# Rotary embedding on one core: first store of 4 and 12 rows, and a load that waits for a multiplication

## The chip, the core and the metric

The kernel runs on one core of a Trainium2 chip. The metric is the device time of one execution in microseconds (us). Three runs of the kernel before gave 161.43, 161.47 and 161.59 us; their median is 161.47.

## What is computed

`x` has shape (16, 512, 16, 64) in float32: batch, sequence, heads, dim. `cos` and `sin` have shape (512, 32), one row for each place in the sequence. Only the first 32 of the 64 numbers are turned, with the first 16 columns of `cos` and `sin`; the other 32 pass through.

```
x1, x2 = x[..., :32], x[..., 32:]
first  = x1[..., :16] * cos[..., :16] - x1[..., 16:] * sin[..., :16]
second = x1[..., :16] * sin[..., :16] + x1[..., 16:] * cos[..., :16]
out    = concatenate([first, second, x2])
```

All of `x` is read once and all of `out` is written once, 33.55 MB each.

## The kernel before

The 8192 positions (batch times sequence) are cut into T = 4 tiles. Each tile gives every one of the 128 partitions K = 16 consecutive rows (positions) of 16 heads by 64 numbers, so that one partition of a tile is 64 KB of contiguous memory and a tile is 8 MB. A ring of NS = 3 tiles (L46) lies in on-chip memory; tile t uses place t % 3, and a tile is worked where it lies and stored from there. Tile 3 therefore takes the place of tile 0, and its load waits until the stores of tile 0 have landed.

`load` (L55) and `store` (L58) each issue one DMA for rows `lo` to `hi` of a tile. All go through SP's queue (`nc.sync`), in the order of the program, but for the tables (L64, L65) and the store of tile 2 (L136), which POOL issues. A DMA issue that must wait stops what stands behind it on the same queue.

At the start the tables go out, then the loads of tile 0, tile 1 and rows 8 to 15 of tile 2 (L66 to L68). VectorE (DVE in the profile) spreads the tables over the partitions (L74 to L86). Then `rotate` (L91) works pieces of tiles, all on VectorE. For rows `lo` to `hi` it issues four instructions: the product with sin into `b_t` (L97), the product with cos in place (L98), the subtraction for the first quarter (L99) and the addition for the second (L106). With `cut`, the addition is issued in two pieces, so that something can wait for the first of them. It returns the subtraction and the list of additions.

`hold` (L114) makes a transfer wait for one VectorE instruction, beyond what its data need.

The order of the work (L124 to L141): tile 0 in two halves of 8 rows (KC = 8), the second with the addition cut after row 11 (KP = 12). The store of tile 0's first half waits for that first piece of the addition; the store of its second half follows, then the load of tile 2's rows 0 to 7, and the load of tile 3. Tile 1 is worked in two halves and stored; that store waits for the subtraction `near` of tile 2's rows 0 to 4 (KM = 5). Tile 2 is worked rows 8 to 15 first, then rows 0 to 4, then rows 5 to 7, and stored by POOL. Tile 3 is worked in two halves and stored.

Of the kernel before, what the change touches and what calls it, by code (L numbers as in the profile page):

```python
# [1 line left out]

# [4 lines left out]


@with_exitstack
def kernel(  # L10
    ctx: ExitStack,
    tc: tile.TileContext,
    x: bass.AP,
    cos: bass.AP,
    sin: bass.AP,
    out: bass.AP,
):
    nc = tc.nc
    fp32 = mybir.dt.float32
    P = 128  # L20
    B, S, H, D = x.shape
    Q = D // 4
    HF = D // 2

    K = 16
    T = B * S // (P * K)
    PB = S // K
    REP = P // PB  # L30
    R = H * D
    NS = 3
    KC = K // 2
    KM = 5
    KP = K - 4

    xf = x.rearrange("b s h d -> (b s h d)").rearrange("(t p f) -> t p f", t=T, p=P)
    of = out.rearrange("b s h d -> (b s h d)").rearrange("(t p f) -> t p f", t=T, p=P)
    cosf = cos.rearrange("(p k) j -> p (k j)", k=K)
    sinf = sin.rearrange("(p k) j -> p (k j)", k=K)  # L40

    const_pool = ctx.enter_context(tc.tile_pool(name="const", bufs=1))
    b_pool = ctx.enter_context(tc.tile_pool(name="bp", bufs=1, space=bass.MemoryType.PSUM))


    ring = const_pool.tile([P, NS, K, H, D], fp32)  # L46
    stage = const_pool.tile([P, 2, K, HF], fp32)
    spun = const_pool.tile([P, 2 * K, Q], fp32)
    packed = const_pool.tile([PB, 2 * K, Q], fp32)
    table = const_pool.tile([P, 2, K, 2, Q], fp32)  # L50

    def rows(t, lo, hi):
        return ring[:, t % NS, lo:hi].rearrange("p k h d -> p (k h d)")

    def load(t, lo=0, hi=K):  # L55
        return nc.sync.dma_start(out=rows(t, lo, hi), in_=xf[t, :, lo * R : hi * R])

    def store(t, lo=0, hi=K, queue=nc.sync):  # L58
        return queue.dma_start(out=of[t, :, lo * R : hi * R], in_=rows(t, lo, hi))  # L59


    nc.vector.memset(stage[:, :, :, 0:Q], 0.0)  # L62
    spread = stage.rearrange("(j b) t k i -> j b t (k i)", b=REP)
    nc.gpsimd.dma_start(out=spread[:, 0, 0], in_=cosf)  # L64
    nc.gpsimd.dma_start(out=spread[:, 0, 1], in_=sinf)  # L65
    load(0)  # L66
    load(1)
    load(2, KC, K)  # L68

    PQ = PB // REP
    nc.vector.stream_shuffle(  # L74
        out=spun[:],
        in_=stage.rearrange("p t k j -> p (t k) j")[:, :, 0:Q],
        mask=[j % PQ * REP for j in range(PB)],
    )
    for q in reversed(range(REP)):
        n = PQ * (q + 1)  # L80
        nc.vector.tensor_copy(out=packed[0:n], in_=spun[q * PB : q * PB + n])  # L81

    for r in range(REP):
        nc.vector.tensor_copy(  # L84
            out=table[r * PB : (r + 1) * PB].rearrange("p t k c j -> p (t k) c j"),
            in_=packed.unsqueeze(2).to_broadcast((PB, 2 * K, 2, Q)),  # L86
        )
    C = table[:, 0].rearrange("p k c j -> p k (c j)")
    Sn = table[:, 1].rearrange("p k c j -> p k (c j)")

    def rotate(t, lo, hi, cut=None):  # L91
        x1 = ring[:, t % NS, lo:hi, :, 0:HF]
        c = C[:, lo:hi].unsqueeze(2).to_broadcast((P, hi - lo, H, HF))
        s = Sn[:, lo:hi].unsqueeze(2).to_broadcast((P, hi - lo, H, HF))
        b_full = b_pool.tile([P, KC, H, HF], fp32, name="b_t")
        b_t = b_full[:, 0 : hi - lo]
        nc.vector.tensor_mul(out=b_t, in0=x1, in1=s)  # L97
        nc.vector.tensor_mul(out=x1, in0=x1, in1=c)  # L98
        first = nc.vector.tensor_sub(  # L99
            out=x1[:, :, :, 0:Q], in0=x1[:, :, :, 0:Q], in1=b_t[:, :, :, Q:HF]  # L100
        )
        ends = [hi - lo] if cut is None else [cut - lo, hi - lo]
        done = []
        for a, b in zip([0] + ends, ends):
            done.append(
                nc.vector.tensor_add(  # L106
                    out=x1[:, a:b, :, Q:HF],
                    in0=x1[:, a:b, :, Q:HF],
                    in1=b_t[:, a:b, :, 0:Q],
                )  # L110
            )
        return first, done

    def hold(transfer, point):  # L114
        tc.add_manual_dep(
            transfer.ins,
            point.ins.name,
            mybir.DependencyInfo(
                mybir.DependencyClass.Sync, mybir.DependencyReason.DATA
            ),  # L120
            reason="the store follows the loads at the DMA engines",
        )

    rotate(0, 0, KC)  # L124
    _, close = rotate(0, KC, K, cut=KP)
    hold(store(0, 0, KC), close[0])
    store(0, KC, K)
    load(2, 0, KC)
    load(3)
    rotate(1, 0, KC)  # L130
    rotate(1, KC, K)
    behind_loads = store(1)
    rotate(2, KC, K)
    near, _ = rotate(2, 0, KM)
    rotate(2, KM, KC)
    store(2, queue=nc.gpsimd)  # L136

    hold(behind_loads, near)
    rotate(3, 0, KC)
    rotate(3, KC, K)  # L140
    store(3)  # L141


# [1 line left out]
_INS = ['x', 'cos', 'sin']  # L145
_OUTS = [((16, 512, 16, 64), 'float32')]


# [23 lines left out]
```

## Time and profile before

| what | us |
|---|---|
| median of three runs | 161.47 |
| the profiled execution | 161.67 |
| its span, first to last instruction | 159.8 |
| VectorE busy | 113.0 |
| end of VectorE's last addition | 131.3 |
| last store, issue to landing | 27.5 |

The profiled execution's time is 1.87 us longer than its span; the difference is what lies around the first and the last instruction. HBM is read for 33.69 MB and written for 33.55 MB, a mean of 421 GB/s over the span.

How to read the profile: in the timeline a line has the start, the duration, the engine (SPq is SP's queue of DMA issues), the line of the kernel, the operation, the tile written and the tile read with their shapes, and how many instructions were merged. A DMA issue's line is the issuing alone; the transfer goes on after it, and its landing is told separately. In the queue table a line has the number of packets, the MB and the share of 16 engines' span that the packets took.

### The profile page before, as it was taken

How to read it: one execution, taken by the hardware profiler on the slowest of the kernel's cores; microseconds unless marked ns; L12 is line 12 of the kernel's file. 1: busy time of each engine (PE TensorE's matmuls, PEld its weight loads, DVE VectorE, ACT ScalarE, POOL GpSimd, SP SyncE). 2: the span in 40 equal slices, each digit the busy share in tenths (PEclk: the TensorE clock that was granted, in tenths of full speed). 3: DMA queues.
4: the chain of work that ended last, by engine and by line, in shares of the span. 5: the costliest groups of instructions: out<-in, count | busy, mean ns of one | idle time of the engine just before them, and what ended most of it. 6: DMA issues, size and time to landing. Idle time of an engine off the chain costs nothing.

```text
span 159.8 us, 120 instructions
## 1 busy us (share of the span) xinstructions
DVE 113.0 (71%) x48; POOL 1.9 (1%) x7
## 2 busy tenths in 40 slices
DVE  1000959999999999999999999999999980000000
POOL 3000000000000000000000000010000000000000
DMA  7969989899799999999999799996996996996990
GB/s 262 541 262 541 410 377 525 377 410 525 303 467 410 394 484 426 402 402 508 402 525 476 312 525 394 394 525 295 492 525 262 525 508 279 525 508 279 525 508 16
DMA packets 1504, 67.24 MB, mean 421 GB/s; under 512 B 192, under 2 KB 192, under 8 KB 224
## 3 DMA queue, kind: packets, MB, share of 16 engines
q1 hardware_dynamic: 1296, 58.72, 85.4%
q0 software_dynamic: 208, 8.52, 12.3%
HBM read 33.69 MB, written 33.55 MB: 421 GB/s over the span
## 4 chain that ended last, share of the span: by engine, by line
DVE 61%; DMA 14%; issue 5%; DVEq 1%
DVE b_t L97 22%; DVE ring L98 22%; DMA ring<-in_x_dram 14%; DVE ring L106 10%; DVE ring L99 7%; DVEq L167 1%; DVEq L97 0%
## 5 line engine op out<-in xcount | busy, mean ns | idle before, releaser
L97 DVE TENSOR_TENSOR b_t<-ring,table 128x4096 f32<-128x4096 f32 (+2 forms) x9 | 35.6, 3958 | 2.1 <-DMA ring<-in_x_dram 1.9
L98 DVE TENSOR_TENSOR ring<-ring,table 128x4096 f32<-128x4096 f32 (+2 forms) x9 | 35.6, 3950 | 0.3
L99 DVE TENSOR_TENSOR ring<-ring,b_t 128x2048 f32<-128x2048 f32 (+2 forms) x9 | 18.4, 2050 | 0.3
L106 DVE TENSOR_TENSOR ring<-ring,b_t 128x2048 f32<-128x2048 f32 (+3 forms) x10 | 18.4, 1853 | 0.0
L74 DVE LOAD_MASK_SELECT spun<-stage x1 | 0.0, 14 | 14.4 <-DMA stage<-in_sin_dram 14.4
L84 DVE COPY table<-packed 32x1024 f32<-32x1024 f32 x4 | 2.7, 684 | 0.1
L59 POOL DMA_DIRECT2D out_dram<-ring x1 | 0.6, 562 | 101.8 <-DVE ring L106 101.8
L81 DVE COPY packed<-spun 32x512 f32<-32x512 f32 (+3 forms) x4 | 1.7, 416 | 0.1
L62 DVE MEMSET stage<- 128x512 f32 x1 | 0.5, 485 | 0.9 <-PEq L156 0.9
L74 DVE STREAM_SHUFFLE spun<-stage 128x512 f32<-128x512 f32 x1 | 0.7, 721 | 0.0
L64 POOL DMA_DIRECT2D stage<-in_cos_dram x1 | 0.6, 644 | 1.3 <-DVE stage L62 1.3
L65 POOL DMA_DIRECT2D stage<-in_sin_dram x1 | 0.5, 535 | 0.0
L156 POOL MEMSET const-bfloat16-1.0<- 128x1 bf16 x1 | 0.1, 102 | 0.0
L156 POOL MEMSET const-float32-0.0<- 128x1 f32 x1 | 0.1, 99 | 0.2 <-issue 0.2
L156 POOL MEMSET const-float32-1.0<- 128x1 f32 x1 | 0.1, 99 | 0.0
L156 POOL MEMSET const-uint8-127<- 128x1 uint8 x1 | 0.1, 99 | 0.0
## 6 DMA issues: line engine op xcount, KB each, us to landing
ring<-in_x_dram SPq DMA_DIRECT2D x2, 4096.0 KB, 40.8
out_dram<-ring SPq DMA_DIRECT2D x2, 4096.0 KB, 17.4
stage<-in_cos_dram POOLq DMA_DIRECT2D x1, 64.0 KB, 9.0
stage<-in_sin_dram POOLq DMA_DIRECT2D x1, 64.0 KB, 13.4
ring<-in_x_dram SPq DMA_DIRECT2D x3, 28.9
out_dram<-ring SPq DMA_DIRECT2D x2, 31.1
out_dram<-ring POOLq DMA_DIRECT2D x1, 39.6
```

The lines of the kernel that those rows point to most:

```text
L59: return queue.dma_start(out=of[t, :, lo * R : hi * R], in_=rows(t, lo, hi))
L62: nc.vector.memset(stage[:, :, :, 0:Q], 0.0)
L64: nc.gpsimd.dma_start(out=spread[:, 0, 0], in_=cosf)
L65: nc.gpsimd.dma_start(out=spread[:, 0, 1], in_=sinf)
L74: nc.vector.stream_shuffle(out=spun[:], in_=stage.rearrange("p t k j -> p (t k) j")[:, :, 0:Q], mask=[j % PQ * REP for j in range(PB)],)
L81: nc.vector.tensor_copy(out=packed[0:n], in_=spun[q * PB : q * PB + n])
L84: nc.vector.tensor_copy(out=table[r * PB : (r + 1) * PB].rearrange("p t k c j -> p (t k) c j"), in_=packed.unsqueeze(2).to_broadcast((PB, ...
L97: nc.vector.tensor_mul(out=b_t, in0=x1, in1=s)
L98: nc.vector.tensor_mul(out=x1, in0=x1, in1=c)
L99: first = nc.vector.tensor_sub(out=x1[:, :, :, 0:Q], in0=x1[:, :, :, 0:Q], in1=b_t[:, :, :, Q:HF])
L106: nc.vector.tensor_add(out=x1[:, a:b, :, Q:HF], in0=x1[:, a:b, :, Q:HF], in1=b_t[:, a:b, :, 0:Q],)
L167: with _tile.TileContext(nc) as tc:
```

## The change

The first store of tile 0 carries 4 rows (KS = 4) and the second 12, instead of 8 and 8; what the first one waits for stays as it is. The load of tile 2's rows 0 to 7, which is next in SP's queue, is made to wait for the product with cos (the line that is L98 before) of tile 1's rows 8 to 12. For that, tile 1's second half is worked as 5 and 3 rows, and `rotate` returns this product too. Tile 2's rows 0 to 7 are worked as 4 and 4 rows instead of 5 and 3, and the store of tile 1 waits for the subtraction of the 4 rows.

```diff
+    KS = 4
...
-        nc.vector.tensor_mul(out=x1, in0=x1, in1=c)
+        scaled = nc.vector.tensor_mul(out=x1, in0=x1, in1=c)
...
-        return first, done
+        return scaled, first, done
...
     rotate(0, 0, KC)
-    _, close = rotate(0, KC, K, cut=KP)
-    hold(store(0, 0, KC), close[0])
-    store(0, KC, K)
-    load(2, 0, KC)
+    _, _, close = rotate(0, KC, K, cut=KP)
+    hold(store(0, 0, KS), close[0])
+    store(0, KS, K)
+    behind_store = load(2, 0, KC)
     load(3)
     rotate(1, 0, KC)
-    rotate(1, KC, K)
+    near, _, _ = rotate(1, KC, KC + KM)
+    hold(behind_store, near)
+    rotate(1, KC + KM, K)
     behind_loads = store(1)
     rotate(2, KC, K)
-    near, _ = rotate(2, 0, KM)
-    rotate(2, KM, KC)
+    _, near, _ = rotate(2, 0, KS)
+    rotate(2, KS, KC)
     store(2, queue=nc.gpsimd)

     hold(behind_loads, near)
```

## The prediction

> **What bounds the kernel now.** I read the page's busy table first, then its slices, its queue table, the chain, the timeline, SP's own waits, and last the trace's DMA packet records (start, duration and size of each packet).
>
> ```profile
> DVE 113.0 (71%) x48; POOL 1.9 (1%) x7
> ...
> DMA  7969989899799999999999799996996996996990
> ...
> q1 hardware_dynamic: 1296, 58.72, 85.4%
> q0 software_dynamic: 208, 8.52, 12.3%
> ```
>
> The reader is to see that VectorE (DVE) stops at about four fifths of the span, while the two DMA queues together hold 85.4 + 12.3 = 97.7% of 16 engines' time: 0.977 x 159.8 = 156.1 us. The dips in the slices are an artefact of counting a packet where it starts. In the packet records every engine runs packet on packet, the first beginning at 1.75 us and the last ending at 158.44; the last landing is at 158.80 and the span ends 1.0 later. A 64 KB packet takes 2.418 us and a 32 KB one 1.212, reading or writing. So the DMA engines set the end, and the chain on the page, which follows VectorE, misleads: VectorE is done at 131.3 and the last store still needs 27.5 us to land.
>
> ```profile
> 47.64 2.34 DVE L106 TENSOR_TENSOR ring<-ring,b_t 128x1024 f32<-128x1024 f32 x2
> 48.88 1.47 SPq L59 DMA_DIRECT2D out_dram<-ring  x2
> ...
> 50.40 21.85 SPq L56 DMA_DIRECT2D ring<-in_x_dram  x2
> ...
> 63.46 4.43 DVE L97 TENSOR_TENSOR b_t<-ring,table 128x4096 f32<-128x4096 f32 x1
> 67.93 4.42 DVE L98 TENSOR_TENSOR ring<-ring,table 128x4096 f32<-128x4096 f32 x1
> ...
> 76.91 4.43 DVE L97 TENSOR_TENSOR b_t<-ring,table 128x4096 f32<-128x4096 f32 x1
> ...
> 90.35 2.83 DVE L97 TENSOR_TENSOR b_t<-ring,table 128x2560 f32<-128x2560 f32 x1
> 93.22 2.83 DVE L98 TENSOR_TENSOR ring<-ring,table 128x2560 f32<-128x2560 f32 x1
> ...
> 104.44 4.43 DVE L97 TENSOR_TENSOR b_t<-ring,table 128x4096 f32<-128x4096 f32 x1
> ```
>
> This is the timeline around the change. SP sends the two halves of tile 0 from 48.88, the first half of tile 2's load at 50.40, and then stands until 71.9, where tile 3's load goes. The other answer to read is SP's waits:
>
> ```profile
> SPq L56 <- DMA out_dram<-ring: 20.1, 1, 20.1
> ```
>
> Tile 3's load waits 20.1 us for tile 0's stores to land, because it takes their place in the ring of tiles.
>
> Where each transfer ended at the DMA engines (its 4-byte completion packets), for a middle engine and for the last one:
>
> ```
>                       middle   last
> load 2, rows 8-15      51.41   51.86
> store 0, rows 0-7      61.11   61.54
> store 0, rows 8-15     70.88   71.23
> load 2, rows 0-7       80.56   80.96
> load 3                 99.88  100.48
> store 3               157.84  158.44
> ```
>
> By following packet ends into packet starts, the last one is the same engine from 51.86 on; it alone decides. It loses time against the plain packet sum twice: the last packet of load 2 takes 1.458 instead of 1.212 (+0.246, 50.40 to 51.86), the last of load 3 takes 2.596 instead of 2.418 (+0.178, 97.89 to 100.49). Both are changes from reading memory to writing it. At the one change from writing to reading (69.3 to 71.0) it loses nothing, but five leading engines take 1.48 to 1.62 for their last 32 KB written, +0.26 to +0.40, mean 0.33. Those still end ahead of it, so that costs nothing now.
>
> **The change part by part.**
>
> *4 and 12 rows.* Each engine still writes 16 packets: 8 of 16 KB and 8 of 48 KB for 16 of 32 KB. Two 32 KB packets take 2 x 1.212 = 2.424, one of 64 KB 2.418, so a packet costs some 0.006 of its own, and an equal count gives 0. Bounds: 0, and 8 x 0.006 = 0.05 if rows of 48 KB go as two packets. The issue times stay at 48.88 and 50.0, since both waits stay. The smaller first store lasts 8 x 0.61 = 4.9 us from 51.1, the second is issued 1.1 us before that begins; hidden with 6.0 us to spare (1.1 + 4.9), beyond which each us late would be a us of gap.
>
> *The held load.* It waits for the 5-row L98 of tile 1's second half. The first L97 there starts at 63.46; in the 5 and 3 row tile of before, L98 ends 93.22 + 2.83 - 90.35 = 5.70 after such a start. So 69.16, and SP sends 0.03 later, as at 48.85 to 48.88: **69.19 instead of 50.40**. Behind it on SP are load 3, store 1 and store 3. Load 3 can't go before tile 0's stores land at 71.85, so it keeps its time; the others go at 97 and 131. The 1.39 us that SP spent on issuing this load at 50.40 go too, and are worth nothing: it stood until 71.9 anyway.
>
> The queue that was never empty now runs out about then. Without the +0.33 the engines would end tile 0's stores 16 x 1.212 + 0.01 after load 2: 70.49 to 70.99, the last at 71.24. When the first data of a newly sent load flow is shown only at the start: load 0 is issued at 0.74, its first packets begin at 1.75 to 2.84, and end, less 2.418, at 2.45 to 2.98. So 1.71 to 2.24 us from issue to flow, and here 70.90 to 71.43. For the last engine: 0 to 0.19 late, and I take its own start of then, 2.84 - 0.74 = 2.10, so 71.29 and **+0.06**.
>
> To it comes what the turn itself costs. Before, the read was queued 18 us ahead and five engines still lost 0.33; the last engine, turning when the others were already reading, lost none. Now nobody can read ahead, and all 16 turn within half a microsecond, the last among them. Bounds: 0 (as it is now for the last engine) and 0.84, the latter if the first packet's excess at the start (0.53 to 1.08, mean of 14 engines 0.84) comes on top of its latest arrival. I take the nearest row, the five engines that turn without their read in flow: **+0.33**.
>
> The Trainium skill, "DMA: Bandwidth & Descriptors", section "Latency and other measured facts", gives about 600 ns to the first byte of a transfer sent by SP. By that estimate the load would be there at 69.8, ahead of every engine's last write, and the sum would be 0; the row shows 1.01 us to the very first packet of this program and over 2 to the latest. The same page's "Rules for kernel authors" says to issue a DMA early and wait on it late, which speaks against holding a load back; no run shows yet what that is worth here.
>
> *Tile 1's second half as 5 and 3 rows.* Four VectorE instructions more. From the timeline, 8 rows in one take 90.35 - 76.91 = 13.44, as 5 and 3 rows 104.44 - 90.35 = 14.09: **+0.65 on VectorE** from 76.9 on. Tile 2's 4 and 4 for 5 and 3 is again eight instructions: 0. POOL's store 2 goes at 105.4, store 3 at 131.96. Both are hidden: at 131.3 each engine still has two to three packets of store 2, some 7 us, and the first packet of store 3 began only at 136.0. If that cover were gone, 0.65 would stand at the end. Data are in time: load 2's first half lands at 81.4 and is used at 91.0 (9.6 us spare), load 3 at 100.8, used at 105.1 (4.3 spare).
>
> *Store 1's wait.* It follows the subtraction of 4 rows rather than 5. With the mean of the 5 and 3 row forms (2.83 and 1.77; 1.49 and 0.95): 91.00 + 2.34 + 2.34 + 1.22 = 96.90 against 97.59. It lies behind load 3 until 99.8 either way: 0. Bounds -0.18 to +0.18, as the last engine's stall beside it could go or double.
>
> **Sum.** 0 + 0.06 + 0.33 + 0 + 0 = +0.39. The profiled execution took 161.67 us (span 159.8 and 1.87 around it), 0.20 over the median of the runs; so 162.06 for such an execution, and 161.47 + 0.39 = 161.86 for the median.
>
> **The rivals.**
>
> *On time.* The load arrives before the last engine needs it, and the turn costs that engine nothing, as before. For it: 0.06 is all that the start's rows ask, and leaders may lose up to 0.4 free. Against it: those rows are of an idle memory. 161.5, within 0.3.
>
> *The stall goes (the other side).* The +0.246 of the last engine lies from 50.40 to 51.86, exactly while SP pushes the load into a queue that takes it slowly (1.39 us rather than 0.34 to 0.42). If that push delays the engine, it is gone, and with it perhaps the 0.178 at 97.89, where store 1's issue falls. Price: -0.42, so 161.05; the next engines end 0.4 to 0.7 earlier than the last, so there is no more to get. It decides if the held load costs under 0.1. Against it: at 71.9 load 3's issue delays no engine by over 0.13, and the 0.178 needs a change 0.7 us early to matter.
>
> *A longer gap.* A load sent into full write traffic takes longer than in an idle memory. From 71.29 and 0.84 more: +0.06 + 0.84 = +0.90, 162.4. Store 1, issued at 97.59 and flowing at 99.8 without a gap, says that a store's part needs under 2.2; no row has a load so.
>
> *The wait holds nothing.* Not possible: SP stands at that load from 50.4, and the multiplication ends at 69.16.
>
> **How the numbers follow.** Forecast (a gap and turn of 0.33 to 0.6) 0.38; longer gap 0.08; on time 0.35; stall gone 0.19. A measurement of this kernel can tell about 0.2%, 0.32 us, from no change. Slower 0.38 + 0.08 = 0.46, same 0.35, faster 0.19. The range goes from the stall gone, 161.05, to the longer gap, 162.4; the forecast's own is 161.8 to 162.1.
>
> **What would show it.** In the packet records: the first packet of load 2's rows 0-7 lasting 1.5 us and more, and the last engine's end of that load at 81.3 instead of 80.96. In the timeline: SP's load at 69.2, VectorE's end at 131.9. I am wrong if the last engine passes 71.2 without a gap (on time), if its packet at 50.40 falls to 1.21 (stall gone), or if another engine comes last.

## The result and the profile after

The changed kernel takes 163.51 us in the median of six runs (162.97 to 165.29), beside 161.47 before: a ratio of 1.014, with a 95% interval of 1.011 to 1.017. It is slower, as forecast, but by 2.04 us in the medians and not by 0.39, and outside the range. Its times also spread over 2.3 us, where those before spread over 0.2.

The page of the changed kernel, the lines that answer to those shown of before:

```profile
DVE 113.5 (70%) x52; POOL 1.9 (1%) x7
...
DMA  7969969959999998899999699899899898899890
...
q1 hardware_dynamic: 1296, 58.72, 85.2%
q0 software_dynamic: 208, 8.52, 12.2%
```

The bound is the same: 85.2 + 12.2 = 97.4% of 161.4 us are 157.2 us of packets on each engine, 1.1 more than before (156.1) for the same bytes and the same number of packets. So the engines hardly stood empty more than before; some packets took longer.

SP's issues in the timeline (start, duration; two merged DMAs each), and what SP waited for:

```profile
48.83 1.48 SPq L60 DMA_DIRECT2D out_dram<-ring  x2
69.12 2.87 SPq L57 DMA_DIRECT2D ring<-in_x_dram  x2
96.85 35.41 SPq L60 DMA_DIRECT2D out_dram<-ring  x2
```

```profile
SPq L57 <- DVE ring L99: 18.8, 1, 18.8
SPq L57 <- DMA out_dram<-ring: 2.1, 1, 2.1
```

The load went at 69.12 (forecast 69.19) and store 1 at 96.85 (forecast 96.92): the order of events came as worked out. Tile 3's load waits 2.1 us instead of 20.1 and goes at 71.7 (71.9 before); the wait only changed its name.

Where the time is lost is seen by stretches. The columns are the stretch, its length, busy time of VectorE and POOL, the clock, the DMA share and GB/s; a packet counts whole where it starts. Before, then after:

```profile
70.50:75.00 4.50, 4.47 (x3) 0.00 (x0) 1.00 1.08 466
75.00:97.00 22.00, 21.79 (x8) 0.00 (x0) 1.00 0.99 429
97.00:101.50 4.50, 4.43 (x4) 0.00 (x0) 1.00 1.08 466
```

```profile
70.50:75.00 4.50, 4.43 (x4) 0.00 (x0) 1.00 1.03 386
75.00:97.00 22.00, 21.76 (x11) 0.00 (x0) 1.00 1.03 445
97.00:101.50 4.50, 4.43 (x3) 0.00 (x0) 1.00 1.16 451
```

The share tells how long the packets took, the GB/s how much they carried. Where the queue turns from tile 0's stores to the load (70.5 to 75), 466 GB/s fell to 386 at nearly the same share. Where it turns from load 3 to store 1 (97 to 101.5), the share rose from 1.08 to 1.16 while less was carried. Between the two (75 to 97) no packets were slow. In the packet records, with the ends told as in the prediction's table, the changed kernel has:

```
                      middle   last    against before
load 2, rows 0-7       81.12   81.69   +0.56  +0.73
load 3                100.92  101.78   +1.04  +1.30
store 3               158.88  159.74   +1.04  +1.30
```

The last engine lost 0.73 at the first turn, 0.57 more at the second and nothing afterwards. Of the profiled execution's own 163.22 - 161.67 = 1.55 us, 1.30 are thus placed; the other 0.25 lie behind the last completion. The first turn slowed not only the load's first packets but also its second ones (32 KB, 1.212 us elsewhere). Of the 16 first packets, which started at 70.6 to 71.1, 12 were slow by over 0.1 us, up to 0.97; of the 16 second ones 11 were, from 71.9 to 72.6, by up to 0.84. At the second, 15 of 16 last packets of load 3 were slow: 2.96 us in the mean, not 2.418.

### The profile page after: what moved, and what is told of

The parts are those of the page before. It is cut to its first block, busy times and chain, and to the rows that moved or that the text cites. A ratio compares the mean times of both kernels' runs of the same rounds, so it can differ in the third digit from the quotient of the medians.

```text
span 161.4 us, 123 instructions
## 1 busy us (share of the span) xinstructions
DVE 113.5 (70%) x52; POOL 1.9 (1%) x7
## 3 DMA queue, kind: packets, MB, share of 16 engines
q1 hardware_dynamic: 1296, 58.72, 85.2%
q0 software_dynamic: 208, 8.52, 12.2%
## 4 chain that ended last, share of the span: by engine, by line
DVE 62%; DMA 14%; issue 4%; DVEq 1%
DVE b_t L98 22%; DVE ring L99 22%; DMA ring<-in_x_dram 14%; DVE ring L107 10%; DVE ring L100 7%; DVEq L170 1%; DVEq L98 0%
## 5 line engine op out<-in xcount | busy, mean ns | idle before, releaser
L98 DVE TENSOR_TENSOR b_t<-ring,table 128x4096 f32<-128x4096 f32 (+3 forms) x10 | 35.8, 3579 | 2.1 <-DMA ring<-in_x_dram 1.8
L99 DVE TENSOR_TENSOR ring<-ring,table 128x4096 f32<-128x4096 f32 (+3 forms) x10 | 35.7, 3571 | 0.3
L100 DVE TENSOR_TENSOR ring<-ring,b_t 128x2048 f32<-128x2048 f32 (+3 forms) x10 | 18.6, 1860 | 0.3
L107 DVE TENSOR_TENSOR ring<-ring,b_t 128x2048 f32<-128x2048 f32 (+3 forms) x11 | 18.6, 1698 | 0.0
```

Source lines behind the costliest of these rows:

```text
L99: scaled = nc.vector.tensor_mul(out=x1, in0=x1, in1=c)
L100: first = nc.vector.tensor_sub(out=x1[:, :, :, 0:Q], in0=x1[:, :, :, 0:Q], in1=b_t[:, :, :, Q:HF])
L107: nc.vector.tensor_add(out=x1[:, a:b, :, Q:HF], in0=x1[:, a:b, :, Q:HF], in1=b_t[:, a:b, :, 0:Q],)
```

## The experiments

**Theory A**: two turns of the DMA queue pay, each for itself: the load comes too late at the first, store 1 too early at the second. **Rival B**: the held load makes everything, the second being its consequence. **Rival C**: the stores' sizes, or the split on VectorE. The ratios below are to the kernel before in runs on the same chip (medians 161.62 and 161.63). A difference given with a sign is the ratio less one, times 161.6 us; it need not be that of the medians, above all where a few runs are long. In the code shown, lines that only pass on or take one more result of `rotate` are left out.

### One part alone

Stores of 4 and 12 rows alone (store412):

```diff
-    hold(store(0, 0, KC), close[0])
-    store(0, KC, K)
+    hold(store(0, 0, 4), close[0])
+    store(0, 4, K)
```

> The kernel before with one part of the change: tile 0's stores as 4 and 12 rows. Theory A (two turns of the DMA queue pay: +0.7 where the held load comes late, +0.6 where store 1 is queued too early) expects 161.5, within 0.2, since the same 16 packets per engine are written and the queue stays full. Rival B (the held load alone makes everything, the later stalls being its consequence) also 161.5. Rival C (the sizes of the stores change the turn at 50 us, where eight engines instead of three were slowed in the changed kernel) expects 161.8 or more, with the last engine's end of load 2's rows 8-15 behind 52.0.

161.93 us, ratio 1.002 (1.0005 to 1.0034): 0.3 us more than expected. But not for rival C's reason: the last engine ended load 2's rows 8-15 at 51.79, not behind 52.0, and store 3 at 158.27, which is 0.17 earlier than before. The 0.3 us lie outside the span, where no view shows them: time less span is 2.15 to 2.25 us in all ten runs, against 1.77 to 1.87 for the kernel before beside them. The changed kernel, which has the same stores, has only 1.74 to 1.82 there, so these 0.3 us are no part of its loss. What makes them stays open.

The split alone (split_only):

```diff
-    rotate(1, KC, K)
+    rotate(1, KC, KC + KM)
+    rotate(1, KC + KM, K)
```

> The kernel before with tile 1's second half as 5 and 3 rows, nothing held; store 1 still waits for the subtraction of 5 rows and so goes 0.65 later, at 98.24, about 1.6 us ahead of load 3's end instead of 2.3. Theories A and B expect 161.5, within 0.2: VectorE's 0.65 lies beside a full queue; A adds that the last packets of load 3 should be no slower than before, as the store comes later. If VectorE's 0.65 were on the path, 162.1.

161.78 us, ratio 1.0013 (1.0003 to 1.0023). No last packet of load 3 was slow. VectorE's 0.65 us do not come through; about 0.2 does.

The held load, with the split that it needs (hold_only):

```diff
-    load(2, 0, KC)
+    behind_store = load(2, 0, KC)
...
-    rotate(1, KC, K)
+    point, _, _ = rotate(1, KC, KC + KM)
+    hold(behind_store, point)
+    rotate(1, KC + KM, K)
```

> The kernel before with the load held by the multiplication of 5 rows and tile 1's second half as 5 and 3 rows; stores as 8 and 8, store 1 behind the 5-row subtraction, so some 2.3 us ahead of load 3's end as before. Theory A expects +0.7, 162.2: the first two packets of load 2's rows 0-7 slow, the last engine at 81.7 instead of 80.96, but the last packets of load 3 hardly slow. Rival B expects the whole +2.0, 163.5, with slow last packets of load 3 too.

162.69 us, ratio 1.0079 (1.0053 to 1.0105), or +1.28 us: between the two, nearer to A's. By stretches:

```profile
70.50:75.00 4.50, 4.43 (x4) 0.00 (x0) 1.00 1.03 379
75.00:97.00 22.00, 21.76 (x10) 0.00 (x0) 1.00 1.03 447
97.00:101.50 4.50, 4.43 (x4) 0.00 (x0) 1.00 1.08 466
```

The first turn is as bad as in the changed kernel (379 GB/s), the second as good as before (share 1.08 at 466). B had asked for a slow second turn here. Of the load's first packets 12 were slow by over 0.1 us, of its second ones 15.

Store 1's earlier point alone (near4_only):

```diff
-    near, _ = rotate(2, 0, KM)
-    rotate(2, KM, KC)
+    _, near, _ = rotate(2, 0, 4)
+    rotate(2, 4, KC)
```

> The kernel before with store 1 waiting for the subtraction of 4 rows, tile 2's rows 0-7 being worked as 4 and 4: the store goes at about 96.25, 3.6 us ahead of load 3's end, as in the changed kernel. Theory A expects +0.6 or more, 162.1, with the last packet of load 3 slow on most engines. Rival B expects 161.5.

162.38 us, ratio 1.0056 (1.0041 to 1.0071), +0.90 (0.76 by the medians). The mirror image, with the issue's line of the timeline below it:

```profile
70.50:75.00 4.50, 4.46 (x3) 0.00 (x0) 1.00 1.09 466
75.00:97.00 22.00, 21.79 (x9) 0.00 (x0) 1.00 0.99 429
97.00:101.50 4.50, 4.43 (x3) 0.00 (x0) 1.00 1.20 466
```

```profile
96.39 35.41 SPq L59 DMA_DIRECT2D out_dram<-ring  x2
```

The same 466 GB/s at a share of 1.20 instead of 1.08: the same packets took a ninth longer. All 16 last packets of load 3 were slow, 2.96 us in the mean. Rival B as it stands falls: the second turn pays without a held load. (A part of it comes back below.)

### How the two prices depend on time

The changed kernel with store 1 behind the 5-row subtraction again (undo_near4):

```diff
-    _, near, _ = rotate(2, 0, KS)
-    rotate(2, KS, KC)
+    _, near, _ = rotate(2, 0, KM)
+    rotate(2, KM, KC)
```

> The changed kernel with store 1 behind the subtraction of 5 rows again (tile 2 worked as 5 and 3): it goes at about 98.2, some 2.2 us ahead of load 3's end, instead of 3.6. Theory A (the two turns of the queue add up: about +1.1 from the held load, +0.8 from store 1 queued too early) expects 162.7, as the kernel with the held load alone, with no slow last packets of load 3. Rival B (the early store matters only in an undisturbed queue) expects 163.5, as the changed kernel.

162.54 us, ratio 1.0079 (1.0045 to 1.0112), as A expected. Its profiled execution was one of its long ones, 163.77 us: a single engine's first packet of the load started late (at 72.29, where the others' start at 70.60 to 70.96) and took 2.04 us instead of 1.21. It ended that load at 82.79 when all the others were done by 81.1, and was still behind at the end, 160.30 against 158.18 in the middle. Its last packet of load 3 began at 99.70, 1.6 us behind store 1's issue at 98.07, and was the only slow one of the 16 (2.64 us). The runs of the three kernels that hold the load to 69 spread by 1.6 to 2.3 us; all others, the kernel before in its longer series among them, by 0.1 to 1.1. That such a late engine makes the long runs of the changed kernel too is likely but not shown: only one execution of each is profiled.

The load held by the product with sin, 2.8 us sooner (hold_early; beside the held load's kernel, as the next):

```diff
+        sined = nc.vector.tensor_mul(out=b_t, in0=x1, in1=s)
...
+    _, _, _, point = rotate(1, KC, KC + KM)
+    hold(behind_store, point)
```

> The kernel with the held load alone, but the load waits for the product with sin of the 5 rows, so that SP sends it at 66.3 instead of 69.2, some 4.5 us ahead of the end of tile 0's stores. If the cost is that of a load that comes too late to be read ahead (theory A), it goes: 161.7, as the split alone, and the first two packets of load 2's rows 0-7 are as fast as before. If the second packet is slow because load 3 is issued beside it at 71.8 (rival D), it stays slow, some 0.4 us, 162.1. If any load that is queued after the stores have begun pays (rival E), 162.6.

161.84 us, ratio 1.0016 (1.0006 to 1.0025): the same as the split alone. The issue's line of the timeline, and the stretch of the first turn, where both slow packets are gone:

```profile
66.37 5.93 SPq L56 DMA_DIRECT2D ring<-in_x_dram  x2
```

```profile
70.50:75.00 4.50, 4.43 (x4) 0.00 (x0) 1.00 1.08 466
```

466 GB/s is the figure of before. So it is the lateness that is paid, not the wait, and E falls. Rival D (load 3's issue at 71.8 slows the second packet) falls too. Load 3 went 0.25 us later here than in the held kernel, 71.97 against 71.72, but in all traces together, of second packets that began 0.2 to 0.6 us behind load 3's issue, 27 of 27 were slow by over 0.1 us where the load was held to 69, and 2 of 48 where it was sent sooner.

The load held by the subtraction, 1.4 us later (hold_late):

```diff
+    _, point, _ = rotate(1, KC, KC + KM)
+    hold(behind_store, point)
```

> The kernel with the held load alone, but the load waits for the subtraction of the 5 rows, so that SP sends it at 70.65, 1.4 us later. Theory A expects each us later to be a us of empty queue: 162.65 + 1.4 = 164.1. If the cost at 69.2 is a fixed price of the turn and not lateness, 162.7.

164.41 us, ratio 1.0177 (1.0162 to 1.0192), 1.7 above the load held to 69.2 by the medians. Yet this is not one us for each us at one place. The issues in the timeline, and the stretches:

```profile
70.62 1.25 SPq L56 DMA_DIRECT2D ring<-in_x_dram  x2
98.16 34.08 SPq L59 DMA_DIRECT2D out_dram<-ring  x2
```

```profile
70.50:75.00 4.50, 4.43 (x4) 0.00 (x0) 1.00 0.91 342
75.00:97.00 22.00, 21.76 (x10) 0.00 (x0) 1.00 1.05 454
97.00:101.50 4.50, 4.43 (x4) 0.00 (x0) 1.00 0.78 233
```

Now the engines stand idle between the stores' end (70.6 to 71.1) and the load's first packets (71.6 to 72.4), and the middle engine ends the load at 82.03, 0.96 behind the kernel held to 69.2. The rest is lost at the second turn: store 1 still goes at 98.16 by VectorE's clock, but load 3 is now late, so its last packets start at 98.8 to 99.2, behind store 1's issue, and take 3.50 us in the mean. One late transfer made the next one early.

From issue to first packet this load took 0.98 to 1.78 us. The Trainium skill, "DMA: Bandwidth & Descriptors", section "Latency and other measured facts", has about 600 ns to the first byte; the trace's figure is the longer one.

Store 1 without a wait for tile 2 (store1_free):

```diff
-    hold(behind_loads, near)
```

> The kernel before without store 1's wait for tile 2: it goes when tile 1 is done, at 76.9, 23 us ahead of load 3's end. If a store queued so early that the engines read it ahead of the last load packets slows just these (theory A: one packet of read-ahead), the price is that of the 4-row wait, which was 3.6 us ahead: 162.4, with the last packets of load 3 slow by about 0.5. If the price grows with the time that the store is queued (rival F), 163 or more.

162.35 us, ratio 1.0048 (1.0033 to 1.0063), as A expected. Its issue in the timeline, and the stretch of the second turn:

```profile
76.83 54.77 SPq L59 DMA_DIRECT2D out_dram<-ring  x2
```

```profile
97.00:101.50 4.50, 4.43 (x4) 0.00 (x0) 1.00 1.22 466
```

The full 466 GB/s at the highest share of all: 16 slow packets, 3.05 us in the mean. Queued 20 us or 1 us ahead of these packets costs the same, so rival F falls.

### Closing the sum, and a try to do better

The changed kernel without the load's wait (undo_hold):

```diff
-    hold(behind_store, near)
```

> The changed kernel without the load's wait (all else as changed): the load is queued from 51.8 on. Theory A expects the slow first packets of load 2's rows 0-7 to go, and of the +2.0 what the other parts make: store 1 goes at 96.9, before the last packets of load 3 begin (97.2 to 97.9), though less far before than with the 4-row wait alone (96.4), so 162.2 to 162.6. Rival B (all from the held load) expects 161.9 at most, the price of the store's sizes and of the split.

162.56 us, ratio 1.0042 (1.0025 to 1.0059). The stretches of the two turns:

```profile
70.50:75.00 4.50, 4.43 (x4) 0.00 (x0) 1.00 1.09 466
...
97.00:101.50 4.50, 4.43 (x3) 0.00 (x0) 1.00 1.10 466
```

The first turn is whole again; eight of 16 last packets of load 3 are slow, by less (2.52 us in the mean), with store 1 at 96.92. Rival B's 161.9 at most is exceeded. Yet B has a share: store 1 goes at the same time as in the changed kernel, but here the last packets of load 3 begin only 0.44 to 0.89 us behind it, there 0.75 to 1.75, because the held load has put them back. So the late load makes the early store worse. How much is not sure: the runs lie in two groups, 161.87 and 162.06, and five of 162.55 to 162.71, and the profiled execution is the one of 162.06.

Tile 0's first store later (store0_later), store 1 later (store1_later), and both (both_later):

```diff
-    KP = K - 4
+    KP = K - 2
...
-    near, _ = rotate(2, 0, KM)
+    _, parts = rotate(2, 0, KM, cut=2)
+    near = parts[0]
```

> The kernel before with tile 0's addition cut after row 13 instead of 11, so that its first store goes at 49.4 instead of 48.9. If a store that is queued before the last load packets begin (49.9 to 50.4) slows them, as theory A has it at 97 us, later is better: the +0.25 of the last engine's packet at 50.4 shrinks, 161.4. If the store then comes too late for the first engines, whose load ends at 51.1, they pay up to 0.3 but are not the last: no change, 161.6.

> The kernel before with store 1 waiting for the first 2 rows of the 5-row addition, so that it goes at 98.2 instead of 97.6, after the last packets of load 3 have begun on all engines but the last. Theory A expects the +0.18 of the last engine to go: 161.45. If nothing is to be got there, 161.6.

> The kernel before with both later points, 49.4 and 98.2. Theory A expects the two gains to add, 161.2 to 161.3, faster than both kernels. If the last engine is behind for another reason than these two turns, 161.6.

161.45 (0.999, 0.9981 to 1.0000), 161.59 (0.9996, 0.9986 to 1.0007) and 161.61 us (0.9993, 0.9984 to 1.0002). The traces do what A says: with both, no last load packet is slow at 50 or at 97, and the last engine ends at 158.09 instead of 158.44. The issues in the timeline, and the second turn:

```profile
49.35 0.94 SPq L59 DMA_DIRECT2D out_dram<-ring  x2
...
98.13 33.55 SPq L59 DMA_DIRECT2D out_dram<-ring  x2
```

```profile
97.00:101.50 4.50, 4.43 (x5) 0.00 (x0) 1.00 1.08 466
```

But the time does not follow: 0.35 us less at the engines, no difference in the runs that the intervals could tell. Some 0.1 us of it comes back outside the span, where the ten runs with both have 1.90 to 1.97 us against 1.76 to 1.86 before. No version here is clearly faster than the kernel before.

The turn at 50 us, from load 2's rows 8-15 to tile 0's first store, shows the early store's effect too, though weaker. In the twelve traces whose first store went at 48.7 to 49.1, it was issued 0.75 to 1.54 us before the last packets of that load began, and of these 16 packets 2 to 13 were slow by over 0.05 us, none by over 0.37. In the two traces with the store at 49.35 and 49.62, 0.27 to 1.00 us before, none was slow.

Eight of the kernels, by store 1's issue and the last packets of load 3 (2.418 us when nothing slows them):

```
                store 1   packets start   mean us   slow of 16
store1_free      76.83    97.27-97.77      3.05       16
near4_only       96.39    97.16-97.95      2.96       16
changed          96.85    97.59-98.59      2.96       15
undo_hold        96.92    97.36-97.81      2.52        8
before           97.59    97.39-97.89      2.43        1
hold_late        98.16    98.77-99.17      3.50       16
store1_later     98.17    97.26-97.75      2.42        0
hold_only        98.26    97.88-98.72      2.42        0
```

What decides is the distance and not the clock (at 98.16 the packets are slow, at 98.17 not). Over all traces but that of the freed store, 208 last packets: where store 1 was issued 0.6 us or more before the packet starts, 53 of 55 are slow (2.45 us and more); at 0.5 to 0.6, three of seven; at less, or when the packet had started, one of 146, which is the last engine of the kernel before. The distance does not settle how slow: at 0.6 to 0.9 us the packets of undo_hold took 2.43 to 2.83 us, those of hold_late 3.07 to 3.78.

## Why the prediction was wrong

**What held.** The bound, the two issue times to within 0.1 us, the turn from writing to reading as a place where time is lost, and that VectorE's extra 0.65 us would be hidden (0.2 of it was not).

**The step that failed: store 1's wait.** "It lies behind load 3 until 99.8 either way: 0. Bounds -0.18 to +0.18." Alone it costs 0.90 us. I had the +0.178 of one engine before me and read it as a fault of that engine. It was probably the edge of an effect: its packet started at 97.89, 0.3 us behind store 1's issue, those of the others at 97.4 to 97.7 around it, and with store 1 at 98.17 it was gone; but four packets of other traces at 0.44 to 0.48 us were not slow. Issued 1.2 us earlier (near4_only), the store reached all 16 packets, issued 0.7 earlier (undo_hold) eight, and in the changed kernel, where load 3 was also late, 15. That a transfer behind others in a queue can't act before its turn was the false assumption; the row that spoke against it was among the two stalls that I had listed. I also held load 3 to 99.8 while my own sum moved it; it ended at 100.92 in the middle. Why a queued store slows the load ahead of it, no view shows; that the engine already reads the store's data is a guess.

**The term that was mis-sized: the held load.** The turn was priced +0.06 + 0.33. The held load alone measured +1.28, about 1.07 without the split. The mechanism was right, by hold_early (gone) and hold_late (worse), and the row was wrong: the five leading engines' 0.33 is that of an engine whose read was queued all along. The upper bound was the better guess, 0.06 + 0.84 = 0.90, beside 0.85 for the last engine in the held kernel's trace (81.81 against the 80.96 of before). I priced a slow first packet; the second ones were slow too.

**The sizes of the stores**: priced 0 to 0.05. Alone they measured 0.3 (0.1 to 0.55), all outside the span and not explained, but the changed kernel does not have these 0.3 us.

**The sum.** In per cent: held load without the split 0.66, split 0.13, store 1's point 0.56, together 1.35, against 1.4 (1.1 to 1.7). Without store 1's point 0.79 is left, as with the held load alone (0.79). Without the load's wait 0.42 (0.25 to 0.59) is left, less than 0.13 + 0.56 = 0.69. That fits the eight slow packets there: with the split, store 1 goes half a us later than in near4_only (96.92 against 96.39), and it is the held load that puts the last packets of load 3 back again. So the parts come to the whole, but the two turns are not independent: store 1's lead was 0.77 to 1.56 us alone and 0.75 to 1.75 in the changed kernel, which is chance. The forecast had only the first of the two large parts, at a third of its size.

**The rivals.** "A longer gap", at 0.08 the least of them, came near the first turn with its 0.90, in part by luck, since slow first and second packets made it up and hardly a gap; and it was blind to the second turn like the others. "The stall goes" rested on the push at 50.40. In hold_only that push is gone and ten packets were slow there instead of three; with the first store at 49.62 the push stays (1.17 us) and none was slow. So the push was not the cause.

## What to carry to other kernels

In this kernel a DMA queue that hardly ever ran empty still lost time at its turns between reading and writing, and the time of issue decided it. A load behind stores wants to be queued well ahead (4.3 us before the first engine ended its stores was as free as 20, 1.4 was not). A store behind a load wants to come no more than 0.5 us before the last load packets start; later still, up to 0.9 us after, brought no gain that the runs could tell. A wait on another engine's progress fixes a time, but what counts is the distance to the packets ahead in the queue: every shift of that queue changes it. The Trainium skill, "DMA: Bandwidth & Descriptors", section "Rules for kernel authors", says to issue a DMA early and wait late; the load agrees with that (held to 69.2: +0.8%, of which 0.13 is the split's), the store does not (freed to 76.8: +0.5%).

## What the hardware showed beyond that

A store waiting in the queue slowed the last 64 KB load packet of all 16 engines from 2.42 to about 3.0 us, no matter whether it had waited 1 or 20 us. A load that came just in time behind stores (issued at 69.2, 1.4 us before the first engine ended its stores) had slow first packets on 5 to 12 of 16 engines and slow second ones on 11 to 15, in three traces, and in one of them one engine started it 1.3 us behind the last of the others. The run times of the three kernels with such a load spread over 1.6 to 2.3 us.
